# Retention matmuls split by row half, square sums written to other tiles, and a re-cut last stage in a one-core layer kernel

## The chip, the cores and the metric

The kernel runs on one core of one Trainium2 chip. The metric is the device time of one launch in microseconds. Three runs of the kernel before gave 1774.49, 1774.91 and 1778.44 us, so the median is 1774.91 us.

## What is computed

One layer over 1024 tokens of width 1024: an RMS norm and one wide projection; a gated causal convolution; a retention with 8 heads (key width 64, value width 128, chunks of 128 tokens); their mixture with an output projection; a mixture of 32 experts, two per token; a small embedding projection ("ple") gated by the normed state; and a final norm. The part that the change touches most is the retention, and the gate at the end:

```python
def step(state, inp):
    qb, kb, vb = inp
    scores = jnp.einsum('bhid,bhjd->bhij', qb, kb) * decay_mask
    inner = jnp.einsum('bhij,bhjv->bhiv', scores, vb)
    cross = jnp.einsum('bhid,bhdv->bhiv', qb, state) * q_decay[None, :, :, None]
    ...
    return state, inner + cross
...
ple = rmsnorm(p[i] @ w_ple_proj[i], g_ple_post[i])
x = x + jax.nn.sigmoid(rmsnorm(x, g_ple_in[i]) @ w_ple_gate[i]) * ple
return rmsnorm(x, g_final)
```

## The kernel before, in words

**Arithmetic.** Most products take three matmuls (`mm3`, lines 192 to 195): each operand is split into a high part (ScalarE copy, line 188) and a low part (VectorE subtraction, line 189), and high x high, high x low and low x high are added up in PSUM. Retention, transposes and the router use plain fp32 matmuls, which the trace shows as two passes each (transposes as one).

**Stages in the order of the program.** `norm_T` (line 224) norms and transposes one half of 512 tokens, `qkv` (line 251) projects it; this is done for both halves. Then eight `gate_pair` calls run, each with one retention chunk threaded into it: `retention` (line 308) returns four steps (`turned`, `scores`, `outputs`, `close`), and `seven` (line 411) puts them between its products with `issue_after`. Convolution, silu gate, mixture (`mix`), `out_proj` and `router` follow, then `ple` (line 782), the expert loop (lines 1125 to 1138), and the last stage (`fin_sum`, `fin_gate`, `fin_out`, lines 1182 to 1220).

**Retention.** The eight heads lie as four pairs a_ and a parity par: the key rows of parity 0 are partitions 0 to 63, of parity 1 partitions 64 to 127. `scores` does the four pairs of parity 0 and then the four of parity 1, each a matmul over 64 rows with 128 weight columns. `outputs` goes by head groups: for two pairs, two matmuls of scores with values ("inner") per pair, and one matmul over all 128 rows with 256 columns of the state ("cross"), whose other blocks are zero. `kv` (line 369) multiplies keys and values with 64 weight columns; its outputs alternate between the two halves of the PSUM partitions.

**What orders the work.** Each engine takes its instructions in the order that a scheduler fixes at build: it takes ready instructions by their place in the program, with `issue_after` and `high_priority` as the hand's corrections. Tiles of one tag share a fixed number of buffers and get them in the order of the program. The tag `w2k` has 10 buffers of 2 KB per partition; the projection's results `r0`, `r1`, `r2`, the square sums' unused outputs (`xssj` in `sumsq`, line 221; `pj` in `ple`, line 805), `pp` and the results `po` of `ple` all use it, and a buffer that is stored is free when its DMA has landed. The tile `shared` (line 168) holds the retention's state, and later 1028 columns for the router; `V.memset(state, 0.0)` (line 760) stands in `vectors()`, behind both projections. The expert stage's pools take over the memory of the work pool: expert 0's `xl` lies over the first three `w2k` buffers, `rs` over the fourth.

**Expert weights.** 96 weight blocks are loaded by SP through the 8 large buffers (`look`, line 739). Half blocks are split into a ring of three tiles `hls` (line 916). One of the three, `first_hl` ("hc"), is of the large tag; it gets its memory behind the seventh weight block, when `ple`'s `pint` is released. The other two ("ha", "hb") lie where the earlier weight pools were. Before, the order is hc, hb, ha, so expert 0's first half block goes into hc. The first transposes of expert 0 (line 949) and the copies `xh`, `xl` are at `high_priority`.

**Last stage.** The last expert's result `yt` is copied from PSUM by ScalarE (line 988) and scattered by POOL. Per 128 tokens `fin_sum` adds the experts' rows, transposes (line 1193), splits, and squares the row (line 1195); `fin_gate` runs 24 matmuls per half row and four elementwise steps; `fin_out` norms and stores.

Of the kernel before, what the change touches and what calls it, by code (L numbers as in the profile page):

```python
# [75 lines left out]
def tile_kernel(ctx, tc, cst, x, p, g_mix, w_in, conv_w, g_ret, w_out_conv, w_out_ret, w_o, g_moe,  # L76
# [141 lines left out]
    def sumsq(src, name, pool=wk):  # L218
        s = pool.tile([128, 8], F32, name=name, tag="sm", bufs=4)
        j = pool.tile([128, 1024], BF, name=name + "j", tag="w2k", bufs=NW)  # L220
        A.activation(j, src, AF.Square, accum_out=s[:, 0:1])
        return s[:, 0:1]
# [72 lines left out]
    def turn(n):  # L295
        t0 = n * 128
        for b in range(2):
            pt = bank("otp", ("o", "kv")[b])
            for j in range(4):
                pe = T.transpose(pt[:, j], osb[b][:, j], ident).ins  # L300
            ot = w2k("ot").rearrange("p (a b) -> p a b", a=4)
            for j in range(4):
                A.activation(ot[:, j], pt[:, j], AF.Copy, scale=gret[:, 4 * b + j:4 * b + j + 1])
            Y.dma_start(out=od[b * 512:(b + 1) * 512, t0:t0 + 128].rearrange("(a p) t -> p a t", p=128), in_=ot)
        return pe


    def retention(n, ck):
# [19 lines left out]

        def scores(pe):
            for par in range(2):  # L330
                sp = bank("sp", ("tr", "S")[par])
                r = slice(par * 64, par * 64 + 64)
                with tc.issue_after(pe):
                    for a_ in range(4):
                        pe = T.matmul(sp[:, a_], kt[r, a_], qt[r, a_], start=True, stop=True).ins
                sb = w2k("sb").rearrange("p (a b) -> p a b", a=4)
                V.tensor_tensor(sb, sp, caus[:, None, :].to_broadcast([128, 4, 128]), op=OP.mult)
                sm.append(sb)
            return pe

        def outputs(pe):
            for b in range(2):
                op = bank("op", ("o", "tr")[b])
                m_ = 0
                with tc.issue_after(pe):
                    for a_ in (2 * b, 2 * b + 1):
                        for par in range(2):
                            h = 2 * a_ + par
                            pe = T.matmul(op[:, h - 4 * b], sm[par][:, a_], v[:, h * 128:(h + 1) * 128],
                                          start=m_ == 0, stop=first, skip_group_check=True).ins  # L350
                            m_ += 1
                        if not first:
                            pe = T.matmul(op[:, (a_ % 2) * 2:(a_ % 2) * 2 + 2], qt[:, a_],
                                          state[:, a_].rearrange("p (u v) -> p u v", u=2), start=False, stop=True,
                                          skip_group_check=True).ins
                A.activation(osb[b], op, AF.Copy)
# [425 lines left out]
    def ple(wpl, pin):  # L782
# [12 lines left out]
        for t in range(8):  # L795
            pp = pps[t]
            for b in range(2):
                cc = slice(b * 512, (b + 1) * 512)
                a = acc("pa")
                for k in range(2):  # L800
                    r0 = k * 1024 + b * 512
                    mm3(a, pp[:, 0, k], pp[:, 1, k], wpl[:, r0:r0 + 512], wpl[:, 2048 + r0:2560 + r0],
                        k == 0, k == 1)
                j = w2k("pj", BF)[:, 0:512]
                A.activation(j, a, AF.Square, accum_out=ss[:, t, b:b + 1])
                o = w2k("po")
# [109 lines left out]
    hls = [t.rearrange("p (s n) -> p s n", s=2) for t in (first_hl, mt("ha"), mt("hb"))]  # L916
    hls[1:] = hls[:0:-1]
    done = [0]
# [60 lines left out]
    def expert_out(e, ht):  # L979
# [7 lines left out]
        for b in range(2):  # L987
            A.activation(yt[:, b * 512:(b + 1) * 512], o[b], AF.Copy)
        st = P.indirect_dma_start(out=yd, out_offset=bass.IndirectOffsetOnAxis(ap=ii[:, 1, e:e + 1], axis=0),
# [192 lines left out]
    def fin_sum(t, yb):  # L1182
# [3 lines left out]
        for g in range(2):  # L1186
# [5 lines left out]
            for j in range(4):  # L1192
                T.transpose(pt[:, j], yb[:, 3, (g * 4 + j) * 128:(g * 4 + j + 1) * 128], ident)
            split(pt, th[:, g * 4:g * 4 + 4], tl[:, g * 4:g * 4 + 4])
        A.activation(yb[:, 0], yb[:, 3], AF.Square, accum_out=s[:, 0:1])
        V.tensor_scalar(s[:, 0:1], s[:, 0:1], 1.0 / D, EPS, op0=OP.mult, op1=OP.add)
# [3 lines left out]
    def fin_gate(t, c, yb, sg, hT, s):  # L1200
        o = fp.tile([128, 512], F32, name="fo", bufs=4)
        for k in range(8):
            mm3(o, hT[0][:, k], hT[1][:, k], wg[c][0][:, k], wg[c][1][:, k], k == 0, k == 7)
        cc = slice(c * 512, (c + 1) * 512)
        A.activation(sg[:, cc], o, AF.Sigmoid, scale=hT[2])
        V.scalar_tensor_tensor(sg[:, cc], sg[:, cc], prs[:, t:t + 1], yb[:, 2, cc], op0=OP.mult, op1=OP.mult)
        V.tensor_tensor(yb[:, 3, cc], yb[:, 3, cc], sg[:, cc], op=OP.add)
        A.activation(sg[:, cc], yb[:, 3, cc], AF.Square, accum_out=s[:, c:c + 1])

    def fin_out(t, yb, s):  # L1210
        V.tensor_tensor(s[:, 0:1], s[:, 0:1], s[:, 1:2], op=OP.add)
        V.tensor_scalar(s[:, 0:1], s[:, 0:1], 1.0 / D, EPS, op0=OP.mult, op1=OP.add)
        P.tensor_tensor(s[:, 2:3], s[:, 0:1], mh, op=OP.pow)
        for c in range(2):
            cc = slice(c * 512, (c + 1) * 512)
            V.scalar_tensor_tensor(yb[:, 3, cc], yb[:, 3, cc], s[:, 2:3], gf[:, cc], op0=OP.mult, op1=OP.mult)
            if t == 7:
                Y.dma_start(out=out[t * 128:(t + 1) * 128, cc], in_=yb[:, 3, cc])
        if t < 7:
# [47 lines left out]
```

## Time and profile before

| | us |
|---|---|
| median of three runs | 1774.91 |
| the profiled execution's own time | 1771.04 |
| its span (first to last instruction) | 1769.2 |
| TensorE busy in the span | 1708.2 |
| mean granted TensorE clock | 0.990 |

The terms of the prediction come from the profiled execution, whose span is 1.8 us less than its time; that time is 3.9 us below the median. "PE" is TensorE's matmuls, "PEld" its weight loads, DVE VectorE, ACT ScalarE, POOL GpSimd, SP the queue that issues most DMAs. A matmul's duration in a timeline overlaps with its neighbours'; the distance from one start to the next is what it costs.

### The profile page before, as it was taken

What the parts mean: (1) busy time and instruction counts of PE and PEld (TensorE: products, weight loads), DVE (VectorE), ACT (ScalarE), POOL (GpSimd) and SP (SyncE); (2) the same over time, 40 slices, a digit from 0 to 9 for tenths busy, and PEclk for the clock granted to TensorE, in tenths of its full rate; (3) what the DMA queues carried; (4) which work ended last, traced back from release to release, by engine and by line L of the source; (5) the groups of instructions that cost most, each with busy time, mean ns of one, the idle gap of its engine ahead of it and who ended that gap; (6) DMA issues with size and microseconds to landing.
All of it is one profiled execution on the core that took longest, in us unless ns stands there. A gap on an engine that the chain in (4) does not pass through costs nothing.

```text
span 1769.2 us, 22046 instructions
## 1 busy us (share of the span) xinstructions
PE 1708.2 (97%) x8063; PEld 1325.2 (75%) x8063; DVE 1265.4 (72%) x1748; ACT 903.2 (51%) x1326; POOL 157.2 (9%) x157
## 2 busy tenths in 40 slices
PE   6999999999999999999999989999999999999697
PEld 5878788888888787788888866666666666666586
DVE  5559575666766775746455378999999988888674
ACT  4343344444222223524322257788888877778542
POOL 1000000000000000000000012222212121100010
PEclk9999999999999999999999999999999999999899
DMA  7534434444113226657556799999999999996561
GB/s 231 151 104 138 157 120 146 130 135 137 60 60 95 72 86 185 203 180 249 180 166 208 268 297 365 350 374 389 366 381 362 382 362 349 373 395 259 211 255 58
DMA packets 166401, 397.63 MB, mean 225 GB/s; under 512 B 14764, under 2 KB 85492, under 8 KB 140692
## 3 DMA queue, kind: packets, MB, share of 16 engines
q1 hardware_dynamic: 156788, 378.19, 61.3%
q0 software_dynamic: 9504, 18.02, 3.4%
q8 instruction: 64, 1.05, 0.2%
q14 instruction: 45, 0.37, 0.1%
HBM read 344.77 MB, written 57.68 MB: 227 GB/s over the span
## 4 chain that ended last, share of the span: by engine, by line
PE 74%; issue 13%; DMA 6%; DVE 4%; ACT 1%; POOL 0%; SPq 0%; POOLq 0%; DVEq 0%; ACTq 0%
PE y L193 4%; PE y L195 4%; PE y L194 4%; PE qa L193 3%; PE qa L195 3%; PE qa L194 3%; PE g L193 3%; PE g L194 3%; PE g L195 3%; PE u L194 3%; PE u L193 3%; PE u L195 3%; DMA both<-in_w_in_dram 3%; PE sd L193 2%; PE sc L193 2%
## 5 line engine op out<-in xcount | busy, mean ns | idle before, releaser
L930 DVE TENSOR_TENSOR hc<-raw,hc 128x1024 fp32r<-128x1024 f32 x128 | 154.3, 1223 | 20.4 <-ACT hc L928 19.2
L930 DVE TENSOR_TENSOR hb<-raw,hb 128x1024 fp32r<-128x1024 f32 x128 | 153.9, 1219 | 15.5 <-ACT hb L928 14.2
L930 DVE TENSOR_TENSOR ha<-raw,ha 128x1024 fp32r<-128x1024 f32 x128 | 154.1, 1222 | 13.7 <-ACT ha L928 11.7
L188 ACT ACTIVATE pc<-both 128x512 fp32r<-128x512 f32 x120 | 75.1, 629 | 157.4 <-PE sc L195 86.0
L928 ACT ACTIVATE ha<-raw 128x1024 fp32r<-128x1024 f32 x128 | 132.7, 1058 | 26.6 <-PE y L195 15.3
L928 ACT ACTIVATE hb<-raw 128x1024 fp32r<-128x1024 f32 x128 | 132.8, 1057 | 21.2 <-PE u L195 11.6
L928 ACT ACTIVATE hc<-raw 128x1024 fp32r<-128x1024 f32 x128 | 132.5, 1056 | 14.5 <-PE y L195 5.7
L189 DVE TENSOR_TENSOR pc<-both,pc 128x512 fp32r<-128x512 f32 x120 | 82.1, 686 | 27.0 <-ACT pc L188 26.6
L193 PE MATMUL y<-ph,wys 128*128 128x512 f32 x248 | 97.1, 392 | 1.9 <-ACT wys L188 1.9
L195 PE MATMUL y<-ph,wys 128*128 128x512 f32 x248 | 96.5, 390 | 0.0
L194 PE MATMUL y<-pl,wys 128*128 128x512 f32 x248 | 96.5, 389 | 0.0
L188 ACT ACTIVATE wys<-wyr 128x1024 fp32r<-128x1024 f32 x31 | 32.8, 1061 | 99.7 <-PE y L195 79.3
L193 PE MATMUL sd<-sh,pc 128*128 128x512 f32 x192 | 76.2, 397 | 3.8 <-DVE u L454 3.8
L195 PE MATMUL sd<-sh,pc 128*128 128x512 f32 x192 | 74.9, 390 | 0.0
L194 PE MATMUL sd<-sl,pc 128*128 128x512 f32 x192 | 74.8, 390 | 0.0
L189 DVE TENSOR_TENSOR wqs<-wqr,wqs 128x1024 fp32r<-128x1024 f32 x32 | 39.1, 1222 | 49.1 <-ACT wqs L188 49.1
L188 ACT ACTIVATE wqs<-wqr 128x1024 fp32r<-128x1024 f32 x32 | 33.9, 1059 | 70.2 <-PE qa L195 63.8
L769 POOL DMA_INDIRECT xgb<-h2d,ii x32 | 36.2, 1130 | 294.6 <-DVE hd L966 198.5
L188 ACT ACTIVATE pc<-bt 128x512 fp32r<-128x512 f32 x48 | 30.3, 630 | 62.7 <-PE sa L195 25.3
L558 DVE TENSOR_TENSOR msg<-y,msg 128x512 f32<-128x512 f32 x32 | 22.1, 690 | 53.7 <-PE y L195 53.7
L448 ACT ACTIVATE u<-sa 128x512 f32<-128x512 f32 x24 | 14.3, 597 | 84.1 <-PE sa L195 44.8
L193 PEld LDWEIGHTS y<-ph,wys 128*128 128x128 f32 x248 | 46.6, 188 | 12.1 <-ACT wys L188 2.8
(400 smaller groups left out, 4837.4 us busy)
## 6 DMA issues: line engine op xcount, KB each, us to landing
raw<-in_w_exp_gate_dram SPq DMA_DIRECT2D x64, 1024.0 KB, 19.7
raw<-in_w_exp_up_dram SPq DMA_DIRECT2D x64, 1024.0 KB, 17.6
raw<-in_w_exp_down_dram SPq DMA_DIRECT2D x63, 1024.0 KB, 18.8
both<-in_w_in_dram SPq DMA_DIRECT2D x24, 1024.0 KB, 5.7
wqr<-in_w_in_dram SPq DMA_DIRECT2D x32, 512.0 KB, 3.8
qd<-r SPq DMA_DIRECT2D x32, 256.0 KB, 2.4
both<-qd SPq DMA_DIRECT2D x8, 1024.0 KB, 4.8
wyr<-in_w_out_conv_dram SPq DMA_DIRECT2D x16, 512.0 KB, 3.8
```

Of the source, the lines that this page charges most:

```text
L188: a = A.activation(hi, src, AF.Copy)
L189: V.tensor_tensor(lo, src, hi, op=OP.subtract)
L193: T.matmul(o, lh, rh, start=start, stop=False, skip_group_check=skip)
L194: T.matmul(o, lh, rl, start=False, stop=False, skip_group_check=skip)
L195: return T.matmul(o, ll, rh, start=False, stop=stop, skip_group_check=skip).ins
L448: A.activation(u2, a, AF.Copy)
L558: V.tensor_tensor(sg, y, sg, op=OP.mult)
L769: g = P.indirect_dma_start(out=xgs[e % 3], out_offset=None, in_=h2d, in_offset=bass.IndirectOffsetOnAxis(ap=ii[:, 0, e:e + 1], axis=0), bo ...
L928: A.activation(hl[:, 0, q:q + 1024], raw[:, q:q + 1024], AF.Copy)
L930: V.tensor_tensor(hl[:, 1, q:q + 1024], raw[:, q:q + 1024], hl[:, 0, q:q + 1024], op=OP.subtract)
```

## The change

It has eight edits. (1) `sumsq` writes its unused squares into `shared`, not into a `w2k` tile. (2) `scores` alternates the two parities, each with a PSUM bank of its own. (3) `outputs` does the cross products first, as eight matmuls over 64 rows and 128 columns, alternating the parities, and then the inner ones by parity; the order of heads in the copies and stores behind follows. (4) `ple` writes its unused squares into a free part of `pint`. (5) The ring of split weights is hb, ha, hc. (6) Of the last expert's result VectorE copies the second half. (7) `fin_sum` squares behind the high copies; the last half row of the gate is done in two parts of 256 columns, with one more sum; (8) the last store's second half is issued by ScalarE.

```diff
     def sumsq(src, name, pool=wk):
-        j = pool.tile([128, 1024], BF, name=name + "j", tag="w2k", bufs=NW)
-        A.activation(j, src, AF.Square, accum_out=s[:, 0:1])
+        A.activation(shared[:, 0:512].bitcast(BF), src, AF.Square, accum_out=s[:, 0:1])
...
-                A.activation(ot[:, j], pt[:, j], AF.Copy, scale=gret[:, 4 * b + j:4 * b + j + 1])
-            Y.dma_start(out=od[b * 512:(b + 1) * 512, t0:t0 + 128].rearrange("(a p) t -> p a t", p=128), in_=ot)
+                A.activation(ot[:, j], pt[:, j], AF.Copy, scale=gret[:, 2 * j + b:2 * j + b + 1])
+            Y.dma_start(out=od.rearrange("(a u p) t -> u p a t", u=2, p=128)[b, :, :, t0:t0 + 128], in_=ot)
...
         def scores(pe):
+            sp = [bank("sp", ("tr", "S")[par]) for par in range(2)]
+            for a_ in range(4):
+                for par in range(2):
+                    r = slice(par * 64, par * 64 + 64)
+                    with tc.issue_after(pe):
+                        pe = T.matmul(sp[par][:, a_], kt[r, a_], qt[r, a_], start=True, stop=True).ins
...
         def outputs(pe):
+            ops = [bank("op", ("o", "tr")[b]) for b in range(2)]
+            for a_ in range(4) if not first else ():
+                for b in range(2):
+                    r = slice(b * 64, b * 64 + 64)
+                    with tc.issue_after(pe):
+                        pe = T.matmul(ops[b][:, a_], qt[r, a_], state[r, a_, b * 128:b * 128 + 128],
+                                      start=a_ == 0, stop=False, skip_group_check=True).ins
+            for b, op in enumerate(ops):
                 with tc.issue_after(pe):
+                    for a_ in range(4):
+                        h = 2 * a_ + b
+                        pe = T.matmul(op[:, a_], sm[b][:, a_], v[:, h * 128:(h + 1) * 128],
+                                      start=first and a_ == 0, stop=True, skip_group_check=True).ins
...
-                j = w2k("pj", BF)[:, 0:512]
-                A.activation(j, a, AF.Square, accum_out=ss[:, t, b:b + 1])
+                A.activation(pint[:, 3808:4064].bitcast(BF), a, AF.Square, accum_out=ss[:, t, b:b + 1])
...
-    hls[1:] = hls[:0:-1]
+    hls.reverse()
...
-            A.activation(yt[:, b * 512:(b + 1) * 512], o[b], AF.Copy)
+            if b and e == NE - 1:
+                V.tensor_copy(yt[:, 512:1024], o[b])
+            else:
+                A.activation(yt[:, b * 512:(b + 1) * 512], o[b], AF.Copy)
...
-            split(pt, th[:, g * 4:g * 4 + 4], tl[:, g * 4:g * 4 + 4])
-        A.activation(yb[:, 0], yb[:, 3], AF.Square, accum_out=s[:, 0:1])
+            copied = split(pt, th[:, g * 4:g * 4 + 4], tl[:, g * 4:g * 4 + 4])
+        with tc.issue_after(copied):
+            A.activation(yb[:, 0], yb[:, 3], AF.Square, accum_out=s[:, 0:1])
...
     def fin_gate(t, c, yb, sg, hT, s):
+        if (t, c) == (7, 1):
+            for q in range(2):
+                fin_part(t, c * 512 + q * 256, 256, c, q * 256, yb, sg, hT, s, 1 + 2 * q)
+        else:
+            fin_part(t, c * 512, 512, c, 0, yb, sg, hT, s, c)
...
     def fin_out(t, yb, s):
+        if t == 7:
+            V.tensor_tensor(s[:, 1:2], s[:, 1:2], s[:, 3:4], op=OP.add)
...
-                Y.dma_start(out=out[t * 128:(t + 1) * 128, cc], in_=yb[:, 3, cc])
+                (Y, A)[c].dma_start(out=out[t * 128:(t + 1) * 128, cc], in_=yb[:, 3, cc])
```

## Rows read from the trace of the kernel before

**Rows 1.** The page, part 1: busy time and share of each engine.

```profile
PE 1708.2 (97%) x8063; PEld 1325.2 (75%) x8063; DVE 1265.4 (72%) x1748; ACT 903.2 (51%) x1326; POOL 157.2 (9%) x157
```

**Rows 2.** Windows: stretch and length; busy PE, PEld, DVE, ACT, POOL; clock; DMA share, GB/s.

```profile
108.70:113.40 4.70, 1.18 (x8) 0.84 (x8) 2.27 (x4) 4.21 (x7) 0.55 (x1) 0.98 0.59 223
113.40:116.60 3.20, 3.20 (x8) 2.23 (x8) 2.47 (x6) 1.64 (x4) 0.55 (x1) 0.50 0.47 115
...
213.00:427.00 214.00, 214.00 (x1214) 179.47 (x1212) 143.02 (x234) 92.43 (x191) 16.43 (x16) 1.00 0.41 132
...
1055.20:1062.20 7.00, 0.01 (x2) 0.00 (x1) 2.26 (x5) 3.10 (x6) 1.67 (x1) 0.75 1.03 384
1062.20:1065.50 3.30, 3.30 (x7) 1.78 (x8) 1.91 (x3) 0.30 (x1) 0.43 (x3) 0.50 1.00 410
```

**Rows 3.** Waits of PE from 1640 us on: sum in us, times, longest.

```profile
PE fpt L1193 <- DVE yb L1189: 12.0, 1, 12.0
...
PE fo L193 <- ACT fth L188: 0.7, 2, 0.4
```

**Rows 4.** Timeline around the second half's norm: start us, us, engine, line.

```profile
109.23 1.05 ACT L221 ACTIVATE xssj<-xi 128x1024 bf16<-128x1024 f32 x1
...
113.46 0.80 PE L193 MATMUL qa<-wqs,ha 128*128 128x512 f32 x1
```

**Rows 5.** Lines 137 and 760 alone: ns min/median/max, first and last start in us.

```profile
L137 SPq DMA_DIRECT2D xi<-in_x_dram x8: 328/410/495, 0.7 to 20.8; - x8
...
L760 DVE MEMSET shared<- x1: 912/912/912, 1.0 to 1.0; 128x1024 f32 x1
```

**Rows 6.** Chain of waits: the first retention chunk, and a router block later.

```profile
216.65 1.64 PE sp L335 x16
...
221.25 1.78 PE op L349 x16
223.04 1.02 PE kv L369 x16
...
852.84 0.86 PE lp L616 x8
```

**Rows 7.** Timeline of PE and PEld in the third chunk's outputs.

```profile
274.29 0.61 PE L349 MATMUL op<-both,sb 128*128 128x128 f32 x4
...
277.89 1.09 PE L369 MATMUL kv<-both 128*64 128x128 f32 x16
...
277.89 0.85 PEld L369 LDWEIGHTS kv<-both 128*64 128x64 f32 x16 [0.33 <-issue]
```

**Rows 8.** Timeline from 1024 us to the first expert's matmuls.

```profile
1024.96 1.99 ACT L928 ACTIVATE ha<-raw 128x1024 fp32r<-128x1024 f32 x2
...
1058.35 0.60 ACT L805 ACTIVATE pj<-pa 128x512 bf16<-128x512 f32 x1 [4.59 <-DMA pled<-po]
...
1059.79 2.00 ACT L928 ACTIVATE hc<-raw 128x1024 fp32r<-128x1024 f32 x2 [0.76 <-DVE po L807]
...
1061.70 0.80 ACT L188 ACTIVATE xh<-xp 128x352 fp32r<-128x352 f32 x2
...
1063.73 0.22 PEld L195 LDWEIGHTS g<-hc,xl 128*88 128x88 f32 x1 [0.74 <-DVE xl L189]
```

**Rows 9.** DMA issues from 1031 to 1062 us: KB each, median us to landing.

```profile
pled<-po SPq DMA_DIRECT2D x16, 256.0 KB, 6.9
```

**Rows 10.** Waits of POOL from 1055 to 1068 us.

```profile
POOL rs L952 <- DMA pled<-po: 2.9, 1, 2.9
```

**Rows 11.** Timeline of the last expert's result and of the last tile.

```profile
1645.41 1.29 ACT L988 ACTIVATE yt<-y 88x512 f32<-88x512 f32 x2 [2.69 <-PE y L195]
...
1760.13 0.69 DVE L1207 TENSOR_TENSOR yb<-yb,sg 128x512 f32<-128x512 f32 x1
...
1763.49 0.99 SPq L1218 DMA_DIRECT2D out_dram<-yb  x2
```

**Rows 12.** Tile pp alone: a subtraction of half width, ns min/median/max.

```profile
L189 DVE TENSOR_TENSOR pp<-ptp,pp x8: 410/411/418, 1029.4 to 1049.1; 128x256 fp32r<-128x256 f32 x8
```

More of the change, by code (lines that the diff above doesn't have):

```diff
@@ L329, in scores @@
         def scores(pe):
-            for par in range(2):
[L331 to L335, printed above, removed]
+            sp = [bank("sp", ("tr", "S")[par]) for par in range(2)]
[4 more added lines that the diff above has]
+                        pe = T.matmul(sp[par][:, a_], kt[r, a_], qt[r, a_], start=True, stop=True).ins
+            for par in range(2):
                 sb = w2k("sb").rearrange("p (a b) -> p a b", a=4)
-                V.tensor_tensor(sb, sp, caus[:, None, :].to_broadcast([128, 4, 128]), op=OP.mult)
+                V.tensor_tensor(sb, sp[par], caus[:, None, :].to_broadcast([128, 4, 128]), op=OP.mult)
                 sm.append(sb)
@@ L341, in outputs @@
         def outputs(pe):
-            for b in range(2):
-                op = bank("op", ("o", "tr")[b])
-                m_ = 0
-                with tc.issue_after(pe):
[L346 to L355, printed above, removed]
+            ops = [bank("op", ("o", "tr")[b]) for b in range(2)]
[6 more added lines that the diff above has]
+            for b, op in enumerate(ops):
+                with tc.issue_after(pe):
+                    for a_ in range(4):
+                        h = 2 * a_ + b
+                        pe = T.matmul(op[:, a_], sm[b][:, a_], v[:, h * 128:(h + 1) * 128],
+                                      start=first and a_ == 0, stop=True, skip_group_check=True).ins
                 A.activation(osb[b], op, AF.Copy)
@@ L1200, in fin_gate, with fin_part @@
     def fin_gate(t, c, yb, sg, hT, s):
-        o = fp.tile([128, 512], F32, name="fo", bufs=4)
+        if (t, c) == (7, 1):
[3 more added lines that the diff above has]
+            fin_part(t, c * 512, 512, c, 0, yb, sg, hT, s, c)
+    def fin_part(t, c0, n, c, w0, yb, sg, hT, s, i):
+        o = fp.tile([128, 512], F32, name="fo", bufs=4)[:, 0:n]
         for k in range(8):
-            mm3(o, hT[0][:, k], hT[1][:, k], wg[c][0][:, k], wg[c][1][:, k], k == 0, k == 7)
-        cc = slice(c * 512, (c + 1) * 512)
+            mm3(o, hT[0][:, k], hT[1][:, k], wg[c][0][:, k, w0:w0 + n], wg[c][1][:, k, w0:w0 + n], k == 0, k == 7)
+        cc = slice(c0, c0 + n)
         A.activation(sg[:, cc], o, AF.Sigmoid, scale=hT[2])
@@ L1207, in fin_gate @@
         V.tensor_tensor(yb[:, 3, cc], yb[:, 3, cc], sg[:, cc], op=OP.add)
-        A.activation(sg[:, cc], yb[:, 3, cc], AF.Square, accum_out=s[:, c:c + 1])
+        A.activation(sg[:, cc], yb[:, 3, cc], AF.Square, accum_out=s[:, i:i + 1])
     def fin_out(t, yb, s):
+        if t == 7:
+            V.tensor_tensor(s[:, 1:2], s[:, 1:2], s[:, 3:4], op=OP.add)
         V.tensor_tensor(s[:, 0:1], s[:, 0:1], s[:, 1:2], op=OP.add)
```

## The prediction

> **What bounds the kernel now.** I read the page first: TensorE is busy for 1708.2 of 1769.2 us and no other engine comes near [rows 1]. So a microsecond is won in two ways only: TensorE does its work in less time, or it stands still less. Then I read the windows. Over the eight gate pairs with the retention, TensorE is busy for 214.00 of 214.00 us while DVE has 143 and ACT 92 [rows 2]; what its instructions cost there falls on the end in full. Then the few places where it does stand still: behind the first projection (108.70 to 113.40 us, 1.18 us of work), between the small embedding product and the first expert (7.00 us with none), and ahead of the last stage (12.0 us) [rows 2, 3]. Behind the first two the granted clock is 0.50, that is 1.2 instead of 2.4 GHz, for some 3.2 and 3.3 us more [rows 2], so each such gap costs about 1.6 us on top of itself.
>
> **The sum** goes against the profiled execution (1771.04 us, 3.9 below the median); the difference is then taken off the median.
>
> **1. Square sums of the second half: -4.5 us.** The rows of x are issued by 20.8 us, yet the first square of the second half runs at 109.23, behind the projection's last copies [rows 4, 5]. In the program nothing but its w2k tile holds it: w2k tiles are handed out in the order of the program, behind all the projection's results. An instruction without such a tile is taken early: the clearing of the state stands behind both projections and runs at 1.0 us [rows 5]. In `shared` the squares, the scaling and probably the transposes come long before 108 us, into time in which ACT and DVE have room. Then the second half's first matmul, now at 113.46, follows 108.70 within the 1.2 us of work that TensorE has in that window [rows 2], wherever that is done: 113.46 - 109.9 = 3.6, plus up to 1.6 of clock. I take 4.5. Bounds: 5.2, and 0 if the scheduler leaves it. The clearing (0.9 us of DVE) must now follow the last square; it is needed only when the first chunk ends, and DVE's room covers it. SP gets nothing new.
>
> **2. Scores: -5.0 us.** A chunk's scores are 16 passes in 1.64 us, 102 ns each, one row half at a time. The nearest thing that alternates two halves of the array is kv, alternating column halves: 16 passes with 128 columns in 1.02 us, 64 ns each [rows 6]. No row shows alternating row halves. I take kv's figure, because its streams are as long: 8 x (1.64 - 1.02) = 5.0. Bounds: 8 x (1.64 - 0.85) = 6.3 with kv's load time [rows 7], and 0. What waits for the scores (DVE's masking) starts no later, since both banks end together and before the next product ends.
>
> **3. Cross products: -4.4 us.** Outputs take 277.89 - 274.29 = 3.60 us a chunk [rows 7]; without cross, in the first chunk, 1.78 [rows 6]; so cross is 1.82. Behind it stand, by kv's figure, 16 passes in 1.02. New is that the 64-row block now sits between blocks of 128 rows. Going into kv the loads stop for 0.33 us, of which 1.02 - 0.85 = 0.17 is on the path [rows 7]; one more of these a chunk. 7 x (1.82 - 1.02 - 0.17) = 4.4. Bounds: 7 x (1.82 - 0.85) = 6.8, and a loss of 7 x 0.33 = 2.3 if nothing overlaps. The copies, squares and stores behind keep their number and size: nothing. The Trainium skill (TensorEngine Tiling (Array Packing), Tiling Modes) says that different tiles load and multiply side by side, but that a change of the mode drains the engine. The gap of 0.33 us agrees with the second; two full ones a chunk would leave 7 x (1.82 - 0.85 - 0.66) = 2.2 us of this term, and the forecast 2.2 us later.
>
> **4. `pj` without a w2k tile, and the order of the ring: -3.0 us.** The last `pj` waits 4.59 us for a store of `po`; in order behind it on ACT come hc, which holds expert 0's first weights, and xh; TensorE starts at 1062.20 [rows 2, 8]. Afterwards 2.5 tiles an iteration become 1.5, so a store has some 6.7 iterations to land in place of 4: this wait goes. And the first half block goes into hb and the second into ha, which are written by 1027 [rows 8]; hc comes third, 24 matmuls of 512 columns later (5.1 us at 2.4 GHz), which covers its copy of 2.00 us and the subtraction behind it [rows 8]. What is late next is xl: TensorE's third matmul waits for it now too, by 0.74 us [rows 8], and it lies over three of the ten tiles whose stores may still be in flight; such a wait is in the trace (rs, 2.9 us) [rows 10]. A store takes 6.9 us [rows 9], so the last ones, computed near 1055, land at 1062 or behind. Bounds: -7.0 (1055.2, and the 0.80 of xh and as much for xl, gives a start at 1056.8; 1.6 us of slow clock go) and +2.0 (xl waits for the very last store). Three of ten tiles are at stake; I take -3.0. With the raw block released early its load moves up on SP, ahead of stores; that is within the bounds.
>
> **5. The end: -1.6 us.** Two copies of `yt` take 1.29 us one behind the other [rows 11]; side by side 0.65 goes, and the scatter, the reload and TensorE's restart follow it: -0.6 (DVE is free there; bound 0). Squaring behind the high copies ends waits that sum to 0.7 us [rows 3]: -0.5. The half part: four steps behind the last matmul get shorter by about 0.69 - 0.41 = 0.28 each [rows 11, 12], -1.1, and one small sum and 48 matmuls of half width for 24 come in, which no row prices; I take half of the 1.1, with -0.9 and +0.4 as bounds. The last store: SP's two issues (0.99 us) [rows 11] wait for one multiplication each anyway; ACT in its place saves nothing, bounds -0.4 and, as ACT issues no DMA in the kernel before, +1.0.
>
> Sum: -4.5 - 5.0 - 4.4 - 3.0 - 1.6 = -18.5 us, so 1774.9 - 18.5 = **1756.4 us**.
>
> **Rivals.**
> - *The row halves do not overlap.* A router block with 96 streaming columns takes 0.86 us for 8 passes, 107 ns each [rows 6], although cross, at 1.82 us for 8 passes of 256 columns, would make it 85. So a load of 128 weight columns seems to be a floor of some 105 ns, and kv's 64 ns with 64 columns fits that as well. If loads stay in line, 16 of them take 1.7 us: scores gain nothing, cross loses 7 x 0.17 = 1.2. Sum: -4.5 + 1.2 - 3.0 - 1.6 = -7.9, **1767.0 us**. For it: the 107. Against it: two row halves load from different partitions. The Trainium skill (TensorE: Matmul & The Clock Gate, LDWEIGHTS) prices a load by its columns over 1.2 GHz, whatever its rows; the router row agrees, and whether two loads go side by side no row here shows.
> - *The wait at the first expert only changes its owner*, to xl: term 4 gives 0, **1759.4 us**. For it: rs's wait [rows 10].
> - *The squares stay where they are*, for a reason that the program doesn't show: without term 1, **1760.9 us**.
> - *Slower: each change of the row half costs something.* Scores and cross make 64 + 56 = 120 changes. At the 0.17 us that entering kv costs this is +20.4, against -9.1 of the other terms (1, 4 and 5): +11.3, **1786 us**. It decides from 9.1 / 120 = 0.08 us a change. Against it: kv changes its column half with each of its 8 matmuls, and they take 1.02 us together [rows 6].
>
> **Chances.** Forecast 0.51; no overlap 0.25; xl 0.10; squares stay 0.08; slower 0.06. A measurement here can tell 0.2%, 3.5 us. All but the last case and the poor end of the second are faster by more: 0.86 faster, 0.08 same (no overlap together with a failing term 1 or 4), 0.06 slower. The range reaches from the forecast with better bounds of terms 2 to 4 (-25) up to no overlap with term 4 at 0 (-4.9): 1749 to 1770.
>
> **What would show it.** Steps 2 and 3: sp's block near 1.0 us and outputs near 3.0, where the rival shows 1.64 and 3.8. Step 1: xssj below 100 us for the second half, no gap at 109 and full clock at 114. Step 4: no pj wait, the first expert matmul before 1060, and the owner of its wait; hc's split behind hb's and ha's. Step 5: TensorE's gap near 11.4 us and a shorter tail behind the last matmul. If the blocks stay at 102 ns a pass, the forecast is wrong by some 10 us; if TensorE waits at new places in the retention, its premise is.

## The result, and the profile after

The changed kernel takes **1762.78 us** (median of four runs, 1760.3 to 1764.4) against 1775.68 us for the kernel before in the same comparison: ratio 0.9924, 95% interval 0.9906 to 0.9942. The forecast was 1756.4 us, the range 1749 to 1770. The time lies inside it, 6.4 us above the forecast. The profiled execution took 1760.3 us (span 1758.4), that is 10.8 us of span less than the profiled one before.

The page of the kernel after, part 1, answers to [rows 1]: TensorE is busy 9.5 us less, and it still sets the time.

```profile
PE 1698.7 (97%) x8143; PEld 1318.4 (75%) x8143; DVE 1264.9 (72%) x1752; ACT 900.2 (51%) x1328; POOL 161.5 (9%) x157
```

To see where the 10.8 us came from, I took the same landmarks in both traces (the first start and the last end of a kind of matmul) and formed the differences of the stretches between them:

| stretch | before | after | difference | forecast |
|---|---|---|---|---|
| start to first product of the projection | 18.00 | 19.00 | +1.00 | 0 |
| to the first gate product (norm and projection) | 189.76 | 186.87 | -2.89 | -4.5 |
| to the last output product (retention) | 207.50 | 198.40 | -9.10 | -9.4 |
| to the first embedding product | 613.24 | 614.12 | +0.88 | 0 |
| to the last expert product | 617.57 | 617.05 | -0.52 | -3.0 |
| to the first transpose of the last stage | 12.03 | 12.98 | +0.95 | -0.6 |
| to the first gate product of the last stage | 2.32 | 1.80 | -0.52 | -0.5 |
| to the last gate product | 98.16 | 98.34 | +0.18 | with the next |
| to the end of the span | 10.65 | 9.88 | -0.77 | -0.5 |

**The gap of the norm.** The windows answer to [rows 2]. Between the halves TensorE now stands still for 0.3 us, not 3.4, and the clock behind it stays at 1.00 (first window; the second is the retention, the others belong to the first expert). Here the columns are as there:

```profile
111.07:115.70 4.63, 4.32 (x25) 3.02 (x23) 2.51 (x5) 4.60 (x9) 0.55 (x1) 1.00 0.74 276
202.00:416.00 214.00, 212.47 (x1293) 175.72 (x1292) 148.25 (x243) 96.83 (x203) 16.40 (x16) 1.00 0.42 137
...
1044.30:1052.75 8.45, 0.74 (x4) 0.24 (x3) 1.52 (x5) 0.68 (x2) 3.86 (x6) 0.78 1.04 403
1052.75:1055.80 3.05, 3.05 (x7) 1.95 (x8) 0.38 (x1) 1.01 (x2) 0.00 (x0) 0.50 1.03 279
...
1020.00:1054.00 34.00, 26.29 (x147) 20.69 (x146) 22.20 (x65) 13.52 (x42) 7.20 (x9) 0.93 1.00 341
```

Only half of the second half's norm moved, though. Of ACT's timeline here are the second and the third square: two run at 23 and 24 us, two behind 112 us, and the first transposes start at 110.91. `norm_T` starts the third square only behind the copies of the first transposes, which the ring has nothing to do with. Two early squares, with their scaling by 33.9 us, were enough to close the gap.

```profile
24.21 1.06 ACT L220 ACTIVATE shared<-xi 128x1024 bf16<-128x1024 f32 x1
...
112.55 1.07 ACT L220 ACTIVATE shared<-xi 128x1024 bf16<-128x1024 f32 x1
```

**The retention.** The chain of the third chunk (start us, us, what; lines 334, 348 and 354 are scores, cross and inner products) answers to [rows 6, 7]. Scores take 1.09 us in place of 1.64. Cross takes 1.09 and inner 1.98, in sum 3.07 in place of 3.60; kv is as it was. The 16 weight loads of the scores, from the timeline of the loads, take 0.97 us.

```profile
264.86 1.09 PE sp L334 x16
...
268.90 1.09 PE op L348 x16
269.99 1.98 PE op L354 x16
271.97 1.02 PE kv L369 x16
```

```profile
264.78 0.97 PEld L334 LDWEIGHTS sp<-qt,kt 64*128 64x128 f32 x16 [0.35 <-issue]
```

From chunk to chunk the distance is 26.46 us in place of 27.46: 1.00 us less, not 1.08. The missing part lies at the entry to the cross products, which start 0.32 us behind the start of the matmul ahead of them (268.51, 268.83); the outputs of the kernel before started 0.23 us behind it (274.06, 274.29).

**The first expert.** The timeline answers to [rows 8]. No pj waits any more, and TensorE starts on hb 0.34 us behind the transposes. But its third matmul needs xl, and VectorE may write xl only when a store of po has landed. The stop of 7.0 us has become one of 7.37, and half clock follows it again (third and fourth window above).

```profile
1044.68 0.46 PE L193 MATMUL g<-hb,xh 128*88 128x512 f32 x1 [0.34 <-ACT xh L188]
...
1052.17 0.96 DVE L189 TENSOR_TENSOR xl<-xp,xh 128x352 fp32r<-128x352 f32 x2 [6.89 <-DMA pled<-po]
1052.75 0.22 PEld L195 LDWEIGHTS g<-hb,xl 128*88 128x88 f32 x1 [7.84 <-DVE xl L189]
1052.75 0.73 PE L195 MATMUL g<-hb,xl 128*88 128x512 f32 x1 [7.37 <-DVE xl L189]
```

**The end.** The waits of PE over the whole span (sum, times, longest) answer to [rows 3]. The stop ahead of the last stage grew from 12.0 to 13.0 us; the waits for fth fell from 0.7 to 0.4. The second and third row are new stops in the mixing and in the router.

```profile
PE fpt L1195 <- DVE yb L1191: 13.0, 1, 13.0
...
PE oa L193 <- DVE msg L558: 1.4, 1, 1.4
...
PE lp L616 <- DVE h2T L613: 1.0, 1, 1.0
...
PE fo L193 <- ACT fth L188: 0.4, 1, 0.4
```

The timeline of the last expert's result, beside [rows 11], shows why. The first copy starts 0.67 us before the last matmul ends (1635.45), as it did before (1645.41 against 1646.07). So the second was never queued behind it: on VectorE it ends 0.72 us behind the last matmul, on ACT it had been 0.63. The scatter then starts only 0.83 us behind the copy's end.

```profile
1634.78 0.59 ACT L990 ACTIVATE yt<-y 88x512 f32<-88x512 f32 x1 [2.69 <-PE y L195]
...
1635.05 0.40 PE L195 MATMUL y<-hc,tl 128*88 128x512 f32 x1
...
1635.48 0.69 DVE L988 COPY yt<-y 88x512 f32<-88x512 f32 x1 [1.89 <-PE y L195]
1636.09 4.05 DVE L1157 SCALAR_TENSOR_TENSOR fl<-fr,vt,fh 128x512 fp32r<-128x512 f32 x6
1637.00 1.35 POOL L991 DMA_INDIRECT yd<-yt,ii  x1 [6.49 <-DVE fl L1157]
```

### The profile page after: what moved, and what is told of

It reads as the page before. It is cut to its first block, busy times and chain, and to the rows that moved or that the text cites. A ratio compares the mean times of both kernels' runs of the same rounds, so it can differ in the third digit from the quotient of the medians.

```text
span 1758.4 us, 22201 instructions
## 1 busy us (share of the span) xinstructions
PE 1698.7 (97%) x8143; PEld 1318.4 (75%) x8143; DVE 1264.9 (72%) x1752; ACT 900.2 (51%) x1328; POOL 161.5 (9%) x157
## 4 chain that ended last, share of the span: by engine, by line
PE 82%; DMA 7%; DVE 6%; ACT 2%; issue 2%; SPq 0%; POOL 0%; DVEq 0%; POOLq 0%; ACTq 0%
PE y L193 6%; PE y L195 6%; PE y L194 6%; PE g L195 3%; PE g L194 3%; PE g L193 3%; PE u L194 3%; PE u L193 3%; PE u L195 3%; DMA both<-in_w_in_dram 3%; PE qa L194 2%; PE qa L195 2%; PE qa L193 2%; PE sd L193 2%; PE sc L193 2%; PE sd L194 2%
## 5 line engine op out<-in xcount | busy, mean ns | idle before, releaser
L188 ACT ACTIVATE wys<-wyr 128x1024 fp32r<-128x1024 f32 x31 | 32.8, 1060 | 98.5 <-PE y L195 78.5
L188 ACT ACTIVATE wqs<-wqr 128x1024 fp32r<-128x1024 f32 x32 | 33.9, 1058 | 67.7 <-PE qa L195 59.2
L193 PEld LDWEIGHTS y<-ph,wys 128*128 128x128 f32 x248 | 46.6, 188 | 12.3 <-ACT wys L188 2.9
```

What stands on the lines that cost most here:

```text
L188: a = A.activation(hi, src, AF.Copy)
L193: T.matmul(o, lh, rh, start=start, stop=False, skip_group_check=skip)
```

## The experiments

My theory after the comparison: the retention's and the norm's terms are real and arrive at the end; the term at the first expert failed because one tile, xl, lies over ring tiles whose stores are under way; the copy of yt on two engines costs time. Rivals: the new stops in the mixing give part of the retention back; the weights' transfers set the pace of the experts anyway.

### Retention as before

Scores, cross and outputs of the kernel before, in the changed kernel.

```diff
-            for a_ in range(4):
-                for par in range(2):
+            for par in range(2):
+                for a_ in range(4):
...
-            for a_ in range(4) if not first else ():
-                for b in range(2):
...
+                        if not first:
+                            pe = T.matmul(op[:, (a_ % 2) * 2:(a_ % 2) * 2 + 2], qt[:, a_],
...
```

> The changed kernel with scores, cross products and outputs in the order of the kernel before. Theory (the row halves overlap, and what a chunk saves falls on the end in full): the blocks of 16 score passes go back from 1.09 to 1.64 us, the outputs of a chunk from 3.07 to 3.60 us, in sum 8 x 0.55 + 7 x 0.53 = 8.1 us, time 1770 to 1771.5 us. Rival (part of it had been given back behind the retention, where two stops of 1.42 and 0.99 us are new): those two stops go, and the time is only 5 to 6 us above the changed kernel's.

Measured: 1771.41 us, ratio to the kernel before 0.9976 (0.9964 to 0.9989), 8.6 us above the changed kernel. The chain has the old blocks again; one output block of 4 inner passes starts every 0.87 us, with a cross pass pair between:

```profile
265.00 1.64 PE sp L334 x16
...
269.60 0.45 PE op L348 x4
...
270.47 0.44 PE op L348 x4
...
273.11 1.02 PE kv L368 x16
```

From the first gate product to the last output product this run needs 205.92 us, the changed kernel 198.40. So the new order of the retention is worth 7.5 us, that is the 8.1 of the blocks less 7 x 0.09 at the entry to the cross products. The totals say 8.6, each known to some 2 or 3 us. The expectation had 8.1, and what the stretch gained arrives at the end. The stops in the mixing stayed (0.88 and 0.99 us); the rival falls, and with it the idea that a faster retention caused them.

### Squares in ring tiles

```diff
-        A.activation(shared[:, 0:512].bitcast(BF), src, AF.Square, accum_out=s[:, 0:1])
+        j = pool.tile([128, 1024], BF, name=name + "j", tag="w2k", bufs=NW)
+        A.activation(j, src, AF.Square, accum_out=s[:, 0:1])
```

> The changed kernel with the squares of the first norm back in tiles of the w2k ring. Theory (the shared tile let the second half's norm run early, and the same made the start worse): the stop of 3.4 us between the halves and 3.4 us at half clock behind it come back (+4.4), the first transposes start at 8.7 in place of 9.2 us and the clock is full from 21 in place of 25 us (-2.5 to -3.0), so the changed kernel plus 1.5 to 3 us. Rival (the later start has nothing to do with the squares): the start stays at 9.2 and the clock at 25, plus 4.4 us.

Measured: 1768.99 us, ratio 0.9958 (0.9941 to 0.9975), 6.2 us above the changed kernel. The gap and the slow clock are back, for longer than in the kernel before (windows of this run):

```profile
111.13:114.56 3.43, 0.00 (x0) 0.03 (x1) 1.00 (x3) 3.40 (x5) 0.55 (x1) 0.79 0.78 294
114.56:119.90 5.34, 5.34 (x16) 4.31 (x17) 4.39 (x7) 2.45 (x6) 0.55 (x1) 0.50 0.44 129
210.75:215.50 4.75, 4.75 (x13) 3.02 (x13) 3.14 (x6) 2.55 (x5) 0.00 (x0) 0.65 0.16 57
```

From the first projection product to the first gate product it needs 191.08 us, the changed kernel 186.87, and the other runs with the shared tile 185.9 to 186.9. So the edit is worth 4.1 to 5.1 us there. My theory was wrong on the start: this run's first product came at 19.67 us, later than any. In the other runs with the shared tile it came at 17.9 to 19.3. The +1.00 us of the table is therefore a difference between executions, not the change's. The third window shows a second loss: behind the same 1.53 us stop at the end of the projection the clock falls, here and in the kernel before. Of the runs with the shared tile it falls there in one only, so I don't count it to the edit.

### The last expert's copies on one engine

```diff
-            if b and e == NE - 1:
-                V.tensor_copy(yt[:, 512:1024], o[b])
-            else:
-                A.activation(yt[:, b * 512:(b + 1) * 512], o[b], AF.Copy)
+            A.activation(yt[:, b * 512:(b + 1) * 512], o[b], AF.Copy)
```

> The changed kernel with the last expert's two copies of yt back on ACT. Theory from the two traces (the copies did not queue before: the first half was ready 0.65 us earlier; the copy on DVE is 0.1 us longer, and the scatter started 1.56 us behind the last matmul in place of 0.92 and took 1.35 in place of 0.99 us): TensorE's stop ahead of the last stage goes from 12.98 back to 12.0 us, time 1.0 us less than the changed kernel. Rival (the term of the prediction: two engines save 0.6 us): the stop grows to 13.6 us.

Measured: 1761.03 us, ratio 0.9919 (0.9903 to 0.9936). The totals can't tell this from the changed kernel, but the stop can: it is 12.0 us, as the theory said. In the four profiled runs with both copies on ACT it is 11.9, 12.0, 12.3 and 12.5 us, in all the others with the copy on VectorE 12.9 to 13.2. So the copy on VectorE costs 0.4 to 1.3 us. The timeline of ACT in this run, with both copies:

```profile
1635.83 1.29 ACT L987 ACTIVATE yt<-y 88x512 f32<-88x512 f32 x2 [2.69 <-PE y L195]
```

POOL's timeline: the scatter starts 0.29 us behind the second copy, and takes 0.98 us again.

```profile
1637.41 0.98 POOL L988 DMA_INDIRECT yd<-yt,ii  x1 [5.85 <-ACT yt L987]
```

And the waits of PE at the end of the span:

```profile
PE fpt L1192 <- DVE yb L1188: 12.0, 1, 12.0
```

### The last tile: half part, and the store by ACT

Two runs, each with one edit undone and of one execution each. First the gate's last half tile in one part again (`fin_gate` as before):

> The changed kernel with the last half tile of the gate in one part again. Read from the last start of a gate matmul to the end of the span (before 10.65, after 9.88 us). Theory (the half part shortens the four steps behind the last matmul by some 0.2 to 0.3 us each, against one sum more): 10.5 to 10.7 us, and the matmuls from the first to the last of the stage take 98.16 in place of 98.34 us. Rival (the store by ACT saved it): 9.9 us.

Then both stores by SP:

```diff
-                (Y, A)[c].dma_start(out=out[t * 128:(t + 1) * 128, cc], in_=yb[:, 3, cc])
+                Y.dma_start(out=out[t * 128:(t + 1) * 128, cc], in_=yb[:, 3, cc])
```

> The changed kernel with both last stores issued by SP again. From the last start of a gate matmul to the end of the span (before 10.65, after 9.88 us). Theory (SP's second issue waits for its own multiplication, so ACT in its place saves next to nothing): 9.8 to 10.0 us. Rival (SP's first issue of 0.5 us was ahead of the second one): 10.2 to 10.5 us.

Measured from the end of the last gate product (the expectations say its start, which is the same landmark misnamed) to the end of the span: 10.65 us without the half part, as in the kernel before, and 9.88 with the store by SP. Of the ten other runs with the half part eight read 9.88 too, and two 10.05 and 10.21. So the half part carries the whole 0.77 us, the store nothing. The matmuls of the stage did not become shorter without the half part (98.90 us): in that execution the half clock at the start of the stage lasted to 1656.8 us, 4.3 us into it, in the kernel after to 1653.2, 3.0 us into it. So that side expectation stays undecided. The timeline of the tail in the kernel after shows the four steps with 256 columns and the added sum, beside 0.69, 0.75, 0.69 and 0.63 us in the run without:

```profile
1748.60 0.47 ACT L1215 ACTIVATE sg<-fo,f 128x256 f32<-128x256 f32 x1 [0.71 <-PE fo L195]
1749.11 0.49 DVE L1216 SCALAR_TENSOR_TENSOR sg<-sg,prs,yb 128x256 f32<-128x256 f32 x1 [1.76 <-ACT sg L1215]
1749.63 0.42 DVE L1217 TENSOR_TENSOR yb<-yb,sg 128x256 f32<-128x256 f32 x1
1750.09 0.42 ACT L1218 ACTIVATE sg<-yb 128x256 f32<-128x256 f32 x1 [1.01 <-DVE yb L1217]
...
1750.63 0.16 DVE L1222 TENSOR_TENSOR f<-f 128x1 f32<-128x1 f32 x1 [0.57 <-ACT sg L1218]
```

### Moving xl

In the changed kernel the first xl lies over the ring slots of the second last and the fourth last store. By the trace the second last landed at 1052.05 us and the last at 1052.67, and xl started at 1052.17. First I gave xh and xl one set of four buffers:

```diff
-        xh = mw.tile([128, 8, CAP], F32R, name="xh", tag="xh", bufs=2)
-        xl = mw.tile([128, 8, CAP], F32R, name="xl", tag="xl", bufs=2)
+        xh = mw.tile([128, 8, CAP], F32R, name="xh", tag="xx", bufs=4)
+        xl = mw.tile([128, 8, CAP], F32R, name="xl", tag="xx", bufs=4)
...
```

> The changed kernel with xh and xl of the experts handed out in turn from one set of four buffers, so that the first xl lies over the retention's state and one slot of the w2k ring in place of three slots with late stores. Theory (xl's wait for a store of po is the whole remaining stop): the stop of 7.37 us at the first expert falls to under 1 us, the half-clock stretch of 6.83 us behind it (3.4 us lost) goes too, and the time falls by 7 to 10.5 us to some 1753 us. Rival 1 (the next late thing, hc's copy or another tile over the ring, takes the wait over): a stop of 4 us or more with another owner, 1759 to 1763 us. Rival 2 (the expert stage is set by the weights' transfers): the stop goes, but new waits for weights give it back within the stage, and its last matmul stays at 1635 us.

Measured: 1758.77 us, ratio 0.9908 (0.9891 to 0.9924). The expected place was missed: the first xl got the fourth of the buffers, and of the late stores only the fourth last was left under it. The wait shrank with it, from 7.4 to 2.9 us, and 1.5 us of another wait showed, for the gathered rows of expert 0 (waits of PE from 1040 to 1060 us):

```profile
PE g L195 <- DVE xl L189: 2.9, 1, 2.9
PE xp L948 <- DMA xgb<-h2d,ii: 1.5, 1, 1.5
```

Then both in one tile, which comes to lie over the retention's state and one slot without a late store:

```diff
-        xh = mw.tile([128, 8, CAP], F32R, name="xh", tag="xh", bufs=2)
-        xl = mw.tile([128, 8, CAP], F32R, name="xl", tag="xl", bufs=2)
+        xx = mw.tile([128, 2, 8, CAP], F32R, name="xx", tag="xx", bufs=2)
+        xh, xl = xx[:, 0], xx[:, 1]
...
```

> The changed kernel with xh and xl of an expert as the two halves of one tile (two buffers), so that the first xl lies over the retention's state and one slot that the last eight stores of po don't use. The first try to move xl put it over the slot of the fourth last store in place of the second last, and its wait shrank from 7.37 to 2.85 us. Theory (the wait is for the store under xl and for nothing else): no wait for a store is left, TensorE's third matmul of the first expert follows the second within 1.5 us (the copy to xh and the subtraction), and the half-clock stretch of 6.83 us shrinks or goes; ahead of it the transposes may wait 0 to 1.5 us for the gathered rows, as in other runs. Last matmul of the experts 7 to 10 us earlier than the 1635.44 us of the changed kernel, time 1753 to 1756 us. Rival (the weights' transfers set the stage): new waits at L193 or L194 for hb, ha or hc appear behind 1050 us and sum to over 4 us, time above 1758 us.

Measured: **1756.61 us**, ratio 0.9884 (0.9867 to 0.9900), just above the 1753 to 1756 expected. No wait for a store is left; xl follows xh directly. What is late next is the gather, and here it took much of what was won. The waits of PE from 1040 to 1060 us hold nothing else:

```profile
PE xp L948 <- DMA xgb<-h2d,ii: 4.3, 1, 4.3
```

The window behind it is at half clock again:

```profile
1047.49:1053.20 5.71, 5.71 (x18) 3.88 (x19) 1.36 (x3) 2.33 (x4) 2.29 (x5) 0.50 0.94 369
```

Both steps together show the cause: the wait follows the store that lies under xl. The weights' transfers do not set the experts' pace: no new wait for weights came up.

### Order of the ring, and pj

Both on top of xl over the state. First `hls[1:] = hls[:0:-1]` in place of `hls.reverse()`:

> The kernel of the run before it (xl over the state), with the order of the three split tiles as in the kernel before, so that hc is the second to be filled. Theory (hc's two copies of 1.0 us and two subtractions of 1.2 us stand ahead of xh on ACT and of xl on DVE again): the first expert's first matmul starts 2 us later and the xl one 2.4 us later than in that run, time 2 to 3 us more. Rival (the order is free once no store is waited for, since hc's raw block is there long before): within 0.5 us of that run.

Measured: 1759.44 us (1755.06 to 1762.1), ratio 0.9900 (0.9881 to 0.9919): by the totals not to be told from 1756.61. In the trace ACT does hc's two copies for 2.0 us ahead of xh, VectorE 2.36 us ahead of xl, and TensorE stands for 3.1 and 0.4 us (its waits in the same stretch):

```profile
PE g L193 <- ACT xx L188: 3.1, 1, 3.1
PE g L195 <- DVE xx L189: 0.4, 1, 0.4
```

So the order costs TensorE some 3 us here, where nothing else is late; in the run before the gather was as late, and that is why the totals don't show it. This run also tells where one of the new stops comes from: the 0.99 us in the router is gone, and the stop ahead of the embedding product is 1.24 us again, as in the kernel before, in place of 0.68 (waits of PE from 1000 to 1030 us). Both come with the order of the ring.

```profile
PE pa L193 <- ACT pp L188: 1.2, 1, 1.2
```

Then pj back on the ring:

```diff
-                A.activation(pint[:, 3808:4064].bitcast(BF), a, AF.Square, accum_out=ss[:, t, b:b + 1])
+                j = w2k("pj", BF)[:, 0:512]
+                A.activation(j, a, AF.Square, accum_out=ss[:, t, b:b + 1])
```

> The changed kernel with xl over the state, and pj in a tile of the w2k ring again. Theory of the prediction (2.5 ring tiles an iteration instead of 1.5 leave a store too little time): ACT waits for a store of po again by 3 to 5 us ahead of the last squares, xh comes as much later, and the first expert starts 3 to 6 us later than with xl over the state alone, time 1759 to 1763 us. Rival (the gathered rows are as late anyway): the wait at pj is there, but the first expert starts within 1.5 us of that kernel's 4.35 us behind the end of the embedding product, time within 2 us of 1756.6.

Measured: 1763.43 us, ratio 0.9937 (0.9921 to 0.9954). That is 6.8 us more than without, and some 9 us by the two ratios, as the kernel before took 1775.11 us beside this run and 1777.07 beside the other. But the waits of ACT say that this is not pj's own wait, which is 1.5 us. With other tiles on the ring the slots fall otherwise, the very last store now goes out of the slot under xh and xl (it landed at 1053.88 us, the one before it at 1053.26, and xx started at 1054.04), and that wait is 7.5 us:

```profile
ACT xx L188 <- DMA pled<-po: 7.5, 1, 7.5
...
ACT pj L805 <- DMA pled<-po: 1.5, 1, 1.5
```

What decided this run is which store lies under xh and xl. What pj is worth by itself is not shown: its 1.5 us lie on ACT ahead of a wait of 7.5 for another store.

### Both gains, and the gather

xl over the state and yt on ACT:

> The changed kernel with xl over the state and the last expert's two copies of yt on ACT. Theory (the two gains are at different places and add up): TensorE's stop ahead of the last stage is 12.0 us, no wait for a store at the first expert, and 0.3 to 4.4 us of wait for the gathered rows, as it falls; 1.0 us below the kernel with xl over the state alone, 1755 to 1756 us. Rival (one gain hides the other): no better than that kernel's 1756.6 us.

Measured: **1753.5 us** (1751.37 to 1756.84), ratio 0.9887 (0.9870 to 0.9903), a little below the 1755 to 1756 expected. The stop ahead of the last stage is 11.9 us. Up to the last expert this kernel is the same as the one with xl over the state alone, and yet the gather cost 4.3 us there, and here it costs 0.7 (waits of PE from 1040 to 1060 us)

```profile
PE xp L948 <- DMA xgb<-h2d,ii: 0.7, 1, 0.7
```

and the clock stays full (windows of this run):

```profile
1044.25:1052.75 8.50, 7.68 (x37) 5.28 (x37) 5.76 (x10) 6.41 (x10) 3.82 (x6) 1.00 1.04 390
1052.75:1055.80 3.05, 3.05 (x15) 2.01 (x14) 3.05 (x3) 3.03 (x4) 0.00 (x0) 1.00 1.07 341
```

From the first embedding product to the last expert product this execution needs 608.91 us, against 617.05 in the changed kernel and 614.78 with the late gather. The gather's landing is a matter of the single execution. All its time lies in a stretch where the DMA engines are busy throughout (last window of the kernel after: share 1.00). Two more runs, on top of the two gains, took weights out of its way:

```diff
-                late = len(raws) == 8 and h == 1
+                late = len(raws) == 8 and h == 1 or len(raws) == 6 and len(gathers) > 0
```

> The kernel of the run before it (two gains), with the two loads of expert 2's gate weights issued by POOL behind the three gathers in place of by SP ahead of them; SP then issues half of the up weights among the last stores. Theory (from 1020 to 1054 us the DMA engines are busy all the time, 0.95 to 1.05 of them, so the gather's 8 to 13 us to landing are a queue of weights and stores that were issued ahead of it): the transposes start 1 to 3 us earlier against the end of the embedding product, time 1752 to 1755 us. Rival (the gather itself is slow): it still lands 10 us or more after its issue, time as the run before.

Measured: 1754.08 us, ratio 0.9879 (0.9859 to 0.9898). The transposes follow at once; 0.3 and 0.4 us are left for xh and xl. With `len(raws) in (6, 7)`:

> As the run before it, with expert 2's up weights too issued by POOL, so that SP issues only stores of po from the middle of the embedding product on. Theory (a queue of weights ahead of the gather): the first gather lands within 8 us of its issue, the transposes follow the embedding product within 0.5 us, no half-clock stretch of more than 3.5 us behind it; the last expert matmul 5 to 8 us earlier than in the kernel with two gains, time 1748 to 1752 us. Rival 1 (stores, or the gather itself, make it slow): a stop of 2 us or more at the transposes remains. Rival 2 (weights then come too late): new waits at the weights' copies between 1075 and 1130 us give back over 2 us.

Measured: 1755.78 us, ratio 0.9891 (0.9874 to 0.9907), where 1748 to 1752 was expected. The gather's rows are there 6.4 us behind the issue (1035.74, and POOL's copy that waits for them starts at 1042.20), as the theory said. But the copies of hc now come ahead of xh on ACT, and TensorE stands for 3.1 us for xh. POOL's timeline first:

```profile
1042.20 0.18 POOL L951 COPY rs<-xgb 88x1 f32<-88x1 f32 x1 [0.80 <-DMA xgb<-h2d,ii]
```

And ACT's, with hc ahead of xx, the tile that holds xh:

```profile
1045.86 2.00 ACT L927 ACTIVATE hc<-raw 128x1024 fp32r<-128x1024 f32 x2 [0.76 <-DVE po L806]
1047.77 0.80 ACT L188 ACTIVATE xx<-xp 128x352 fp32r<-128x352 f32 x2
```

In these two runs the first gather landed 5.8 and 6.4 us behind its issue, in the other changed kernels, as far as the trace tells, 8.1 to 12.9. So the weights issued ahead of it delay the gather, as far as one profiled execution of each can show, but neither run is faster than the one with two gains. The intervals of the four kernels with xl over the state and the ring reversed all overlap: by the totals they are equally fast. Three of them lie clear of the changed kernel's interval, the fourth touches its end. xl over the state alone is the simplest of them.

## Why the prediction was right or wrong

**Direction and range: right**, and the mechanism of the two largest terms as well. One slip in the sums: the better bounds of terms 2 to 4 make -26.2 us, not -25; the lower end of 1749 belongs to -26.2.

**1 (squares, -4.5): size right, the way only in part.** The gap and the slow clock went. But "nothing but its w2k tile holds it" is true of two of the four squares only, and the transposes, which were to come "long before 108 us", stayed at 110.91. The table shows only -2.89, since the changed execution had its full clock at the start from 25.0 us only, the one before from 21.1. Undone, the edit costs 4.1 to 5.1 us in that stretch.

**2 (scores, -5.0) and 3 (cross, -4.4): mechanism right, sizes high.** Measured 8 x 0.55 = 4.4 and 7 x 0.44 = 3.1, in sum the 7.5 of the run with the old retention; that the table has -9.10 comes from the slow clock at the first gate product, some 1.6 us, which the profiled execution of after did not have. That part is luck. I priced an alternating pass at kv's 64 ns; it is 1.09 / 16 = 68. I priced one change of the block's rows at 0.17 us a chunk; it is two, 0.09 into the cross products and 1.98 - 1.78 = 0.20 behind them.

"No row shows alternating row halves" was wrong, and with it "one row half at a time". The scores of the kernel before put one parity behind the other in the program, but the trace shows the first passes of the second parity beside the last ones of the first. Here are two stretches of 0.11 us of the third chunk's scores, tile sp alone; behind PE and PEld stand the passes and the loads under way. In the first one half is at work, in the second both:

```profile
270.16:270.27 0.11, 0.11 (x3) 0.11 (x3) 0.00 (x0) 1.00 0.81 186
270.49:270.60 0.11, 0.11 (x5) 0.11 (x6) 0.00 (x0) 1.00 0.72 186
```

One half alone starts a pass every 0.11 us; in the changed kernel a pair starts every 0.11 us, its two passes and its two loads 6 or 7 ns apart. So the trace of before could have settled the rival "no overlap", which I gave 0.25: its floor of some 105 ns per load, off the router's row, holds within a half and not across the two. In the changed kernel the PSUM bank alternates with the half, and no run separates the two. The Trainium skill (TensorEngine Tiling (Array Packing), Tiling Modes) says that different tiles load and multiply side by side and that a change of the mode drains the engine: the pairs agree with the first, the 0.09 and 0.20 us with the second, at less than the two full gaps that I had set beside it.

**4 (first expert, -3.0): wrong.** The step that failed is "three of ten tiles are at stake; I take -3.0": a share of tiles is no measure of a wait. xl waits for all of the stores under it, so the latest one alone counts, and that was the second last. The prediction had named xl as next late and "the wait only changes its owner, to xl" as a rival with 0.10; that rival came true, for this term. What I could have seen is that the stores' 6.9 us [rows 9] reach past the transposes for each of the last five or so, so that with three slots under xl a miss was unlikely.

**5 (end, -1.6): half right.** Squaring behind the copies gave -0.52 as forecast, the same in all profiled runs of the change. The half part gave -0.77, within its bounds. The store by ACT gave nothing, as forecast. The copy of yt was wrong in sign: I read "x2, 1.29 us" [rows 11] as a queue of two. But the first was released about 0.65 us before the last matmul had ended, so the second never waited for it. VectorE's copy is also 0.69 us long, and the scatter behind it started later and took longer: +0.95 in place of -0.6.

**Not foreseen:** +0.88 us in the mixing and the router, with two stops of 1.42 and 0.99 us; with the old retention they were there as well (0.88 and 0.99). The 0.99 comes with the order of the ring, which in turn shortens the next stop from 1.24 to 0.68. The 1.42 belongs to the execution: the run with the last store by SP is the same program up to there and has no such stop. And +0.88 is the least that was seen: in the twelve other profiled runs the stretch took 614.7 to 618.1 us, against 613.24 in the one execution of before. How much of that the change costs stays open.

In the traces the change is worth 10.8 us where I had 18.5, and the table says where the 7.7 us are: term 4 2.5, norm 1.6, the copy of yt 1.55, the start 1.0, mixing and router 0.9, the retention 0.3 (1.9 without the luck of the clock). The start and most of the norm's part belong to the one execution that was profiled; by the medians the change is worth 12.9 us.

## What to carry to other kernels

Matmuls that use 64 rows should alternate between the row halves, here each half with a PSUM bank of its own (one bank for both was not tried), and blocks of 64 and of 128 rows should be kept together. Before an overlap is priced by the mean of a block, the single starts inside the block are worth a look: they may already show it. When a ring is relieved, look up which later tiles lie over its slots and which transfer each slot was last used for: the latest one sets the wait, not their number. Two copies of one engine that follow each other in a profile are only a queue if the second was ready before the first ended; a second engine saves nothing otherwise.

## What the runs showed of the hardware

- Alternating row halves bring 16 passes of 128 columns from 1.64 to 1.09 us. Going from blocks of 128 rows into one of 64 and back costs 0.09 and 0.20 us.
- A stop of 1.53 us at the end of the projection was followed by a mean granted clock of 0.62 (207.76 to 212.20 us of the kernel before) and 0.65 (with the squares on the ring), and by 1.00 in the changed kernel (205.87 to 215.50 us). With the last store by SP, a program that is the same up to the last tile, it fell as well (0.64 from 204.62 to 209.20 us). The stop is the same each time; why the clock differs stays open. The stop of 1.7 to 1.95 us at the first product of the mixture is alike: in ten of the 14 profiled executions half clock follows it (0.50 from 732.60 to 735.90 us of the kernel with two gains), in four it doesn't (1.00 from 732.45 to 736.45 us of the kernel after), and the length of the stop doesn't decide it: 1.67 us is among the ten, 1.83 among the four.
- The scatter behind VectorE's copy took 1.35 us in place of 0.98 and started 0.83 in place of 0.29 us behind the copy. VectorE was at work all that time (4.05 us of fl); that this is the reason was not tried.
- The same program up to the last expert had its gather land in time for a stop of 0.7 us in one execution and of 4.3 in another, with the DMA engines full in both.
